# Add, layer normalization, one core: row statistics in two fixed sets of columns, one semaphore update for each four rows, one register value for all waits of a turn

## The chip, the cores and the metric

One core of a Trainium2 chip. The metric is the time of one execution on the device in microseconds (us). All runs told here were fast ones (granted clock 1.0). Before the change the median was 239.73 us of three runs (239.52 to 239.84).

## The reference

```python
# x, residual: float32 [16, 1024, 512]; gamma, beta: [512]; eps = 1e-5
z = x + residual
mean = np.mean(z, axis=-1, keepdims=True)
var = np.var(z, axis=-1, keepdims=True)
return gamma * (z - mean) / np.sqrt(var + eps) + beta
```

16,384 rows lie as 128 "rows" of 128 partitions, 512 values each; one such 128x512 row is 0.262 MB. All of `x` and `residual` is read once, all of the output written once: 100.67 MB.

## The kernel before

SP, POOL, ACT and DVE are engines of the core (SyncE, GpSimd, ScalarE and VectorE). SP issues every large transfer, on one queue. POOL adds `residual` to `x` in place, eight rows at a time. ACT takes the statistics of four rows (a "turn"): four Identity passes that sum into `nm` (minus the mean), four Square passes with that mean as bias that sum into `ssq`, one root. DVE takes two passes over each row, with a reciprocal between them. Each turn's statistics have columns of their own in `[P, total]` arrays, addressed by a register.

```python
Z_ROWS, R_ROWS, STORE_LAG, TURN = 64, 32, 40, 4
OUT_CHUNKS = [16] * 7 + [8, 4, 4]
...
    # SP: loads, and stores as rows are finished; a load into a used part of zbuf waits for its store
    for c, (lo, n) in enumerate(loads_x):
        ...
            wait_rows(s_out, "out", olo + on)
            move(dram(of, olo, on), part(zbuf, Z_ROWS, olo, on), so[oc])
    ...
    with act.Fori(0, turns) as t:
        zoff = act.snap((t * (TURN * D)) % (Z_ROWS * D))
        r0 = act.snap(t * TURN)
        act.wait_ge(s_add, r0 + TURN)
        for k in range(TURN):
            act.activation(out=junk_m[k][:, :], in_=zbuf[:, bass.ds(zoff + k * D, D)],
                           func=ACT.Identity, scale=-inv_d,
                           accum_out=nm[:, bass.ds(r0 + k, 1)]).then_inc(s_act, 1)
        act.wait_ge(s_act, r0 * 2 + TURN)
        for k in range(TURN):
            act.activation(out=junk_s[k][:, :], in_=zbuf[:, bass.ds(zoff + k * D, D)],
                           func=ACT.Square, bias=nm[:, bass.ds(r0 + k, 1)],
                           accum_out=ssq[:, bass.ds(r0 + k, 1)]).then_inc(s_act, 1)
        act.wait_ge(s_act, r0 * 2 + 2 * TURN)
        act.activation(out=std[:, bass.ds(r0, TURN)], in_=ssq[:, bass.ds(r0, TURN)],
                       func=ACT.Sqrt, bias=eps_t[:, 0:1], scale=inv_d).then_inc(s_std, TURN)
    ...
    with dve.Fori(0, turns) as t:
        ...
        dve.wait_ge(s_act, r0 * 2 + 2 * TURN)
        # four passes: row = (row + nm) * gamma
        dve.wait_ge(s_std, r0 + TURN)
        dve.reciprocal(out=rstd[...], in_=std[...]).then_inc(s_dve, TURN)
        dve.wait_ge(s_dve, r0 + TURN)
        # four passes: row = row * rstd + beta, each .then_inc(s_out, 1)
```

Of the kernel before, what the change touches and what calls it, by code (L numbers as in the profile page):

```python
# [8 lines left out]
FP32 = mybir.dt.float32  # L9
ACT = mybir.ActivationFunctionType  # L10
ALU = mybir.AluOpType
# [6 lines left out]
Z_ROWS = 64  # L18
# [5 lines left out]


TURN = 4


EARLY = 2
# [3 lines left out]
def kernel(  # L33
# [9 lines left out]
    nc = tc.nc  # L43
    P = nc.NUM_PARTITIONS
# [3 lines left out]
    N, D = xf.shape  # L48
    inv_d = 1.0 / float(D)
    total = N // P  # L50
    turns = total // TURN


    tc.close()
# [8 lines left out]
    def dram(t, lo, n):  # L63
# [5 lines left out]
    zbuf = nc.alloc_sbuf_tensor("zbuf", [P, Z_ROWS * D], FP32)  # L69
# [1 line left out]
    gb_row = nc.alloc_sbuf_tensor("gb_row", [1, 2 * D], FP32)  # L71
    ones = nc.alloc_sbuf_tensor("ones", [1, P], FP32)
    eps_t = nc.alloc_sbuf_tensor("eps_t", [P, 1], FP32)

    nm = nc.alloc_sbuf_tensor("nm", [P, total], FP32)
    ssq = nc.alloc_sbuf_tensor("ssq", [P, total], FP32)
    std = nc.alloc_sbuf_tensor("std", [P, total], FP32)
    rstd = nc.alloc_sbuf_tensor("rstd", [P, total], FP32)
    gamma_p = nc.alloc_psum_tensor("gamma_p", [P, D], FP32)
    beta_p = nc.alloc_psum_tensor("beta_p", [P, D], FP32)  # L80
    junk_m = [nc.alloc_psum_tensor(f"junk_m{i}", [P, D], FP32) for i in range(TURN)]
    junk_s = [nc.alloc_psum_tensor(f"junk_s{i}", [P, D], FP32) for i in range(6 - TURN)]
    junk_s += [
        nc.alloc_sbuf_tensor(f"junk_s{i}", [P, D], FP32) for i in range(6 - TURN, TURN)
    ]
# [3 lines left out]
    def sem(name):  # L89
        s = nc.alloc_semaphore(name)  # L90
        sems.append(s)
        return s
# [5 lines left out]
    s_const = sem("const")  # L98
    s_pe = sem("pe")
    s_add = sem("add")  # L100
    s_act = sem("act")
    s_std = sem("std")
    s_dve = sem("dve")
    s_out = sem("out")
    so = [sem(f"so{c}") for c in range(len(stores))]
# [3 lines left out]
    def part(buf, size, lo, n):  # L109
        assert lo % size + n <= size  # L110
        return buf[:, (lo % size) * D : (lo % size + n) * D]
# [60 lines left out]
    for c, (lo, n) in enumerate(loads_x):  # L172
        nc.gpsimd.wait_ge(sx[c], 16)
        for rc, (rlo, rn) in enumerate(loads_r):
            if lo <= rlo < lo + n:
                assert rlo + rn <= lo + n
                nc.gpsimd.wait_ge(sr[rc], 16)
                for a in range(rlo, rlo + rn, ADD):
# [3 lines left out]
                        out=z, in0=z, in1=part(rbuf, R_ROWS, a, an), op=ALU.add  # L182
                    ).then_inc(s_add, an)


    act = nc.scalar
    act.preload_act_table_set("sqrt_and_others")  # L187
    act.wait_ge(s_const, 2)
    with act.Fori(0, turns) as t:  # L189
        zoff = act.snap((t * (TURN * D)) % (Z_ROWS * D))  # L190
        r0 = act.snap(t * TURN)
        act.wait_ge(s_add, r0 + TURN)
        for k in range(TURN):
            act.activation(  # L194
                out=junk_m[k][:, :],
                in_=zbuf[:, bass.ds(zoff + k * D, D)],
                func=ACT.Identity,
                scale=-inv_d,
                accum_out=nm[:, bass.ds(r0 + k, 1)],
            ).then_inc(s_act, 1)  # L200
        act.wait_ge(s_act, r0 * 2 + TURN)  # L201
        for k in range(TURN):
            act.activation(  # L203
                out=junk_s[k][:, :],
                in_=zbuf[:, bass.ds(zoff + k * D, D)],
                func=ACT.Square,
                bias=nm[:, bass.ds(r0 + k, 1)],
                accum_out=ssq[:, bass.ds(r0 + k, 1)],
            ).then_inc(s_act, 1)
        act.wait_ge(s_act, r0 * 2 + 2 * TURN)  # L210
        act.activation(  # L211
            out=std[:, bass.ds(r0, TURN)],
            in_=ssq[:, bass.ds(r0, TURN)],
            func=ACT.Sqrt,
            bias=eps_t[:, 0:1],
            scale=inv_d,
        ).then_inc(s_std, TURN)


    dve = nc.vector  # L220
    dve.wait_ge(s_pe, 2)
    with dve.Fori(0, turns) as t:
        zoff = dve.snap((t * (TURN * D)) % (Z_ROWS * D))
        r0 = dve.snap(t * TURN)
        dve.wait_ge(s_act, r0 * 2 + 2 * TURN)
        for k in range(TURN):
            row = zbuf[:, bass.ds(zoff + k * D, D)]
            dve.scalar_tensor_tensor(  # L228
                out=row,
                in0=row,  # L230
                scalar=nm[:, bass.ds(r0 + k, 1)],
                in1=gamma_p[:, :],
                op0=ALU.add,
                op1=ALU.mult,
            )
        dve.wait_ge(s_std, r0 + TURN)
        dve.reciprocal(  # L237
            out=rstd[:, bass.ds(r0, TURN)], in_=std[:, bass.ds(r0, TURN)]
        ).then_inc(s_dve, TURN)
        dve.wait_ge(s_dve, r0 + TURN)  # L240
        for k in range(TURN):
            row = zbuf[:, bass.ds(zoff + k * D, D)]
            dve.scalar_tensor_tensor(  # L243
                out=row,
                in0=row,
                scalar=rstd[:, bass.ds(r0 + k, 1)],
                in1=beta_p[:, :],
                op0=ALU.mult,
                op1=ALU.add,
            ).then_inc(s_out, 1)  # L250


    blks = nc.main_func.blocks
# [43 lines left out]
```

## Time and profile before

| | before |
|---|---|
| time, median of 3 | 239.73 us |
| share of the span that the transfer queue fills | 99.1% of 16 engines |
| ACT busy; one ACT turn of four rows | 78%; 6.21 us |
| DVE busy | 74% |
| last store issued; span | 230.8; 238.4 us |

From the page of the kernel before: the span and instruction count, the load and store queue's share of the 16 transfer engines, the chain that ended last by engine, and three groups (busy us, mean ns of one, then idle us just before them and who ended it):

```profile
span 238.4 us, 1803 instructions
...
q1 hardware_dynamic: 6336, 100.67, 99.1%
...
ACT 38%; DMA 33%; issue 10%; POOL 7%; ACTq 5%; DVE 3%; SPq 1%; DVEq 0%; POOLq 0%
...
L194 ACT ACTIVATE junk_m<-zbuf 128x512 f32 x128 | 74.9, 585 | 28.5 <-POOL zbuf L181 23.3
L203 ACT ACTIVATE junk_s<-zbuf,nm 128x512 f32 x128 | 88.8, 694 | 3.9
L243 DVE SCALAR_TENSOR_TENSOR zbuf<-zbuf,rstd,beta_p 128x512 f32 x128 | 87.1, 744 | 1.1
...
```

The chain gives ACT 38%, more than any other, and ACT is busy 78%. The queue is at 99.1%. To see which binds, compare what a turn costs each: ACT's turn is read from its timeline (start, length, operation, idle before), from one root to the next:

```profile
...
123.18 0.19 ACT L194 ACTIVATION_READ_ACCUMULATOR junk_m<-zbuf  x1
123.49 0.69 ACT L203 ACTIVATE junk_s<-zbuf,nm 128x512 f32 x1
...
126.24 0.19 ACT L203 ACTIVATION_READ_ACCUMULATOR junk_s<-zbuf,nm  x1
126.54 0.30 ACT L211 ACTIVATE std<-ssq,eps_t  x1
127.02 0.60 ACT L194 ACTIVATE junk_m<-zbuf 128x512 f32 x1 [0.18 <-issue]
...
```

The next turn's first Identity starts at 127.02, this turn's started at 120.81: 6.21 us. The last accumulator read ends at 123.37 and the first Square starts at 123.49, a gap of 0.12; the root starts 0.11 after the squares' last read; 0.18 is idle at the loop's end. For the same four rows the transfers need 3 x 4 x 0.262 = 3.15 MB, 7.3 us at the 429 GB/s of the table below. ACT has time to spare, and the waits show it (us in total, times, longest; the longest wait for POOL, 17.5 us, is the one for the first sums of all, and 5.8 us lie after 110 us):

```profile
...
ACT junk_m L194 <- POOL zbuf L181: 23.3, 3, 17.5
...
ACT junk_m L194 <- issue: 5.2, 29, 0.2
...
```

The table by stretches (stretch, its length, then busy us and count of PE, PE loads, DVE, ACT and POOL, the clock, and the last two columns, DMA share and GB/s):

```profile
...
12.00:206.00 194.00, 0.00 (x0) 0.00 (x0) 154.93 (x252) 167.20 (x491) 135.03 (x16) 1.00 1.00 429
206.00:226.00 20.00, 0.00 (x0) 0.00 (x0) 17.38 (x29) 18.05 (x54) 6.97 (x2) 1.00 1.01 436
226.00:236.00 10.00, 0.00 (x0) 0.00 (x0) 4.75 (x8) 0.00 (x0) 0.00 (x0) 1.00 0.98 418
236.00:237.00 1.00, 0.00 (x0) 0.00 (x0) 0.00 (x0) 0.00 (x0) 0.00 (x0) 1.00 0.08 33
237.00:238.00 1.00, 0.00 (x0) 0.00 (x0) 0.00 (x0) 0.00 (x0) 0.00 (x0) 1.00 0.04 16
...
```

The issue of the last store, on SP's timeline:

```profile
...
230.81 0.33 SPq L138 DMA_DIRECT2D out_dram<-zbuf  x1
```

### The profile page before, as it was taken

The page shows a single profiled execution, that of the slowest core. Times are in us where ns is not written, and L with a number is a line of the kernel's source. Part 1 is how long each engine was busy: PE and PEld are TensorE (multiplying, and loading weights), DVE is VectorE, ACT ScalarE, POOL GpSimd, SP SyncE. Part 2 cuts the span into 40 slices and gives each one's busy share as a digit, 9 for nine tenths or more (in the row PEclk, how much of TensorE's full clock was granted, in tenths as well). Part 3 has the DMA queues.
Part 4 walks back from the last instruction along what each step waited for, and adds up shares of the span by engine and source line. Part 5 has one row for each costly group of instructions (what it writes and reads, how often), then busy time and mean ns, then how long its engine had stood idle before and what let it go on. Part 6 is the DMA issues. An engine that isn't in the chain of part 4 may idle for free.

```text
span 238.4 us, 1803 instructions
## 1 busy us (share of the span) xinstructions
PE 3.7 (2%) x4; PEld 1.2 (0%) x4; DVE 177.2 (74%) x290; ACT 186.5 (78%) x545; POOL 142.2 (60%) x21
## 2 busy tenths in 40 slices
PE   0600000000000000000000000000000000000000
PEld 0100000000000000000000000000000000000000
DVE  0000488888888889998888888887888648888870
ACT  2003999999999999999999999989997399999700
POOL 0098988989889407893088930889209892770000
DMA  8999999999999999999999999999999999999996
GB/s 308 438 429 415 437 437 429 426 423 437 429 429 418 440 434 426 459 434 396 429 429 429 434 429 429 426 470 434 390 434 418 434 440 408 472 434 434 390 425 257
DMA packets 6340, 100.67 MB, mean 422 GB/s; under 512 B 706, under 2 KB 706, under 8 KB 708
## 3 DMA queue, kind: packets, MB, share of 16 engines
q1 hardware_dynamic: 6336, 100.67, 99.1%
q10 hardware_dynamic: 4, 0.00, 0.0%
HBM read 67.11 MB, written 33.55 MB: 422 GB/s over the span
## 4 chain that ended last, share of the span: by engine, by line
ACT 38%; DMA 33%; issue 10%; POOL 7%; ACTq 5%; DVE 3%; SPq 1%; DVEq 0%; POOLq 0%
DMA rbuf<-in_residual_dram 21%; ACT junk_s L203 20%; ACT junk_m L194 18%; DMA out_dram<-zbuf 12%; POOL zbuf L181 7%; ACTq L194 2%; DVE zbuf L228 2%; DVE zbuf L243 1%; ACTq L203 1%; SPq L138 1%; ACTq L189 1%; ACT std L211 0%; ACTq L201 0%; ACTq L210 0%; DVEq L228 0%
## 5 line engine op out<-in xcount | busy, mean ns | idle before, releaser
L181 POOL TENSOR_TENSOR zbuf<-zbuf,rbuf 128x4096 f32<-128x4096 f32 (+1 forms) x17 | 142.0, 8353 | 70.9 <-DMA rbuf<-in_residual_dram 70.9
L228 DVE SCALAR_TENSOR_TENSOR zbuf<-zbuf,nm,gamma_p 128x512 f32 x128 | 87.1, 743 | 50.4 <-ACT junk_s L203 50.4
L194 ACT ACTIVATE junk_m<-zbuf 128x512 f32 x128 | 74.9, 585 | 28.5 <-POOL zbuf L181 23.3
L203 ACT ACTIVATE junk_s<-zbuf,nm 128x512 f32 x128 | 88.8, 694 | 3.9
L243 DVE SCALAR_TENSOR_TENSOR zbuf<-zbuf,rstd,beta_p 128x512 f32 x128 | 87.1, 744 | 1.1
L203 ACT ACTIVATION_READ_ACCUMULATOR junk_s<-zbuf,nm x128 | 23.9, 187 | 0.0
L194 ACT ACTIVATION_READ_ACCUMULATOR junk_m<-zbuf x128 | 23.9, 187 | 0.0
L211 ACT ACTIVATE std<-ssq,eps_t x32 | 9.5, 297 | 3.7
L237 DVE RECIPROCAL rstd<-std x32 | 5.4, 170 | 0.0
L187 ACT ACT_TABLE_LOAD x1 | 1.3, 1283 | 2.7 <-PEq L55 2.7
L123 PE MATMUL gamma_p<-gb_row,ones 1*128 1x512 f32 x2 | 2.0, 1122 | 7.3 <-DMA gb_row<-in_gamma_dram 7.3
L123 PE MATMUL beta_p<-gb_row,ones 1*128 1x512 f32 x2 | 1.9, 1056 | 0.0
L118 DVE MEMSET ones<- 1x128 f32 x1 | 0.2, 165 | 2.0 <-PEq L55 2.0
L123 PEld LDWEIGHTS beta_p<-gb_row,ones 1*128 1x128 f32 x2 | 0.7, 332 | 1.0 <-DMA gb_row<-in_beta_dram 0.5
L123 PEld LDWEIGHTS gamma_p<-gb_row,ones 1*128 1x128 f32 x2 | 0.5, 305 | 7.3 <-issue 7.3
L278 POOL MEMSET const-float32-0.0<- 128x1 f32 x1 | 0.1, 99 | 0.2 <-issue 0.2
L278 POOL MEMSET const-bfloat16-1.0<- 128x1 bf16 x1 | 0.1, 101 | 0.0
L278 POOL MEMSET const-uint8-127<- 128x1 uint8 x1 | 0.1, 101 | 0.0
L278 POOL MEMSET const-float32-1.0<- 128x1 f32 x1 | 0.1, 98 | 0.0
L119 DVE MEMSET eps_t<- 128x1 f32 x1 | 0.1, 59 | 0.0
## 6 DMA issues: line engine op xcount, KB each, us to landing
zbuf<-in_x_dram SPq DMA_DIRECT2D x15, 2048.0 KB, 32.8
rbuf<-in_residual_dram SPq DMA_DIRECT2D x15, 2048.0 KB, 30.1
out_dram<-zbuf SPq DMA_DIRECT2D x7, 4096.0 KB, 28.6
zbuf<-in_x_dram SPq DMA_DIRECT2D x2, 1024.0 KB, 32.6
rbuf<-in_residual_dram SPq DMA_DIRECT2D x2, 1024.0 KB, 34.6
out_dram<-zbuf SPq DMA_DIRECT2D x1, 2048.0 KB, 15.0
out_dram<-zbuf SPq DMA_DIRECT2D x2, 1024.0 KB, 9.4
gb_row<-in_gamma_dram ACTq DMA_DIRECT2D x1, 2.0 KB
```

What stands on the lines that cost most here:

```text
L123: nc.tensor.matmul(dest[:, :], ones[:, :], gb_row[:, k * D : (k + 1) * D], start=True, stop=True).then_inc(s_pe, 1)
L138: i = nc.sync.dma_start(out=out, in_=in_).then_inc(s, 16)
L181: nc.gpsimd.tensor_tensor(out=z, in0=z, in1=part(rbuf, R_ROWS, a, an), op=ALU.add).then_inc(s_add, an)
L187: act.preload_act_table_set("sqrt_and_others")
L189: with act.Fori(0, turns) as t:
L194: act.activation(out=junk_m[k][:, :], in_=zbuf[:, bass.ds(zoff + k * D, D)], func=ACT.Identity, scale=-inv_d, accum_out=nm[:, bass.ds(r0 + ...
L203: act.activation(out=junk_s[k][:, :], in_=zbuf[:, bass.ds(zoff + k * D, D)], func=ACT.Square, bias=nm[:, bass.ds(r0 + k, 1)], accum_out=ss ...
L211: act.activation(out=std[:, bass.ds(r0, TURN)], in_=ssq[:, bass.ds(r0, TURN)], func=ACT.Sqrt, bias=eps_t[:, 0:1], scale=inv_d,).then_inc(s ...
L228: dve.scalar_tensor_tensor(out=row, in0=row, scalar=nm[:, bass.ds(r0 + k, 1)], in1=gamma_p[:, :], op0=ALU.add, op1=ALU.mult,)
L237: dve.reciprocal(out=rstd[:, bass.ds(r0, TURN)], in_=std[:, bass.ds(r0, TURN)]).then_inc(s_dve, TURN)
L243: dve.scalar_tensor_tensor(out=row, in0=row, scalar=rstd[:, bass.ds(r0 + k, 1)], in1=beta_p[:, :], op0=ALU.mult, op1=ALU.add,).then_inc(s_ ...
L278: nc = _bacc.Bacc("TRN2", target_bir_lowering=False, num_devices=1)
```

## The change

Its intent: spare ACT and DVE the register work between their instructions. Statistics live in two sets of four columns at fixed addresses; the last row of four alone updates a semaphore; three separate semaphores count rows alike, so that one register value (`due`) serves every wait. As columns are reused, ACT must wait until DVE's reciprocal of two turns back is done. Two turns are written out in each pass of the loop.

```diff
+SETS = 2
+LAP = SETS * TURN
 ...
-    nm = nc.alloc_sbuf_tensor("nm", [P, total], FP32)      # and ssq, std, rstd
+    nm, ssq, std, rstd = (
+        [nc.alloc_sbuf_tensor(f"{name}{j}", [P, TURN], FP32) for j in range(SETS)]
+        for name in ("nm", "ssq", "std", "rstd")
+    )
 ...
-    with act.Fori(0, turns) as t:
-        zoff = act.snap((t * (TURN * D)) % (Z_ROWS * D))
-        r0 = act.snap(t * TURN)
-        act.wait_ge(s_add, r0 + TURN)
 ...
+    act.sem_inc(s_dve, LAP)
+    with act.Fori(0, total // LAP) as lap:
+        z0 = act.snap((lap * (LAP * D)) % (Z_ROWS * D))
+        r0 = act.snap(lap * LAP)
+        for j in range(SETS):
+            due = act.snap(r0 + (j + 1) * TURN)
+            act.wait_ge(s_dve, due)
+            act.wait_ge(s_add, due)
+            zk = [zbuf[:, bass.ds(z0 + (j * TURN + k) * D, D)] for k in range(TURN)]
+            for k in range(TURN):
+                i = act.activation(out=junk_m[k][:, :], in_=zk[k], func=ACT.Identity,
+                                   scale=-inv_d, accum_out=nm[j][:, k : k + 1])
+            i.then_inc(s_mean, TURN)
+            act.wait_ge(s_mean, due)
+            for k in range(TURN):
+                i = act.activation(out=junk_s[k][:, :], in_=zk[k], func=ACT.Square,
+                                   bias=nm[j][:, k : k + 1], accum_out=ssq[j][:, k : k + 1])
+            i.then_inc(s_ssq, TURN)
+            act.wait_ge(s_ssq, due)
+            # root of ssq[j] into std[j], .then_inc(s_std, TURN)
 ... DVE alike: waits s_ssq >= due, s_std >= due,
+            dve.reciprocal(out=rstd[j][:, :], in_=std[j][:, :]).then_inc(s_dve, TURN)
+            dve.wait_ge(s_dve, due + LAP)
 ... second pass over four rows, the last alone:
-            ).then_inc(s_out, 1)
+            i.then_inc(s_out, TURN)
```

More of the change, by code (lines that the diff above doesn't have):

```diff
@@ L50 @@
     total = N // P
-    turns = total // TURN
     tc.close()
@@ L73 @@
     eps_t = nc.alloc_sbuf_tensor("eps_t", [P, 1], FP32)
-    nm = nc.alloc_sbuf_tensor("nm", [P, total], FP32)
-    ssq = nc.alloc_sbuf_tensor("ssq", [P, total], FP32)
-    std = nc.alloc_sbuf_tensor("std", [P, total], FP32)
-    rstd = nc.alloc_sbuf_tensor("rstd", [P, total], FP32)
+    nm, ssq, std, rstd = (
+        [nc.alloc_sbuf_tensor(f"{name}{j}", [P, TURN], FP32) for j in range(SETS)]
+        for name in ("nm", "ssq", "std", "rstd")
+    )
     gamma_p = nc.alloc_psum_tensor("gamma_p", [P, D], FP32)
@@ L100 @@
     s_add = sem("add")
-    s_act = sem("act")
-    s_std = sem("std")
+    s_mean, s_ssq, s_std = sem("mean"), sem("ssq"), sem("std")
     s_dve = sem("dve")
@@ L188 @@
     act.wait_ge(s_const, 2)
-    with act.Fori(0, turns) as t:
-        zoff = act.snap((t * (TURN * D)) % (Z_ROWS * D))
-        r0 = act.snap(t * TURN)
-        act.wait_ge(s_add, r0 + TURN)
-        for k in range(TURN):
-            act.activation(
-                out=junk_m[k][:, :],
-                in_=zbuf[:, bass.ds(zoff + k * D, D)],
-                func=ACT.Identity,
-                scale=-inv_d,
-                accum_out=nm[:, bass.ds(r0 + k, 1)],
-            ).then_inc(s_act, 1)
-        act.wait_ge(s_act, r0 * 2 + TURN)
-        for k in range(TURN):
-            act.activation(
-                out=junk_s[k][:, :],
-                in_=zbuf[:, bass.ds(zoff + k * D, D)],
-                func=ACT.Square,
-                bias=nm[:, bass.ds(r0 + k, 1)],
-                accum_out=ssq[:, bass.ds(r0 + k, 1)],
-            ).then_inc(s_act, 1)
-        act.wait_ge(s_act, r0 * 2 + 2 * TURN)
-        act.activation(
-            out=std[:, bass.ds(r0, TURN)],
-            in_=ssq[:, bass.ds(r0, TURN)],
-            func=ACT.Sqrt,
-            bias=eps_t[:, 0:1],
-            scale=inv_d,
-        ).then_inc(s_std, TURN)
+    act.sem_inc(s_dve, LAP)
@@ new lines @@
+    with act.Fori(0, total // LAP) as lap:
[7 more added lines that the diff above has]
+            for k in range(TURN):
+                i = act.activation(
+                    out=junk_m[k][:, :],
+                    in_=zk[k],
+                    func=ACT.Identity,
+                    scale=-inv_d,
+                    accum_out=nm[j][:, k : k + 1],
+                )
+            i.then_inc(s_mean, TURN)
+            act.wait_ge(s_mean, due)
+            for k in range(TURN):
+                i = act.activation(
+                    out=junk_s[k][:, :],
+                    in_=zk[k],
+                    func=ACT.Square,
+                    bias=nm[j][:, k : k + 1],
+                    accum_out=ssq[j][:, k : k + 1],
+                )
+            i.then_inc(s_ssq, TURN)
+            act.wait_ge(s_ssq, due)
+            act.activation(
+                out=std[j][:, :],
+                in_=ssq[j][:, :],
+                func=ACT.Sqrt,
+                bias=eps_t[:, 0:1],
+                scale=inv_d,
+            ).then_inc(s_std, TURN)
@@ L220 @@
     dve = nc.vector
     dve.wait_ge(s_pe, 2)
-    with dve.Fori(0, turns) as t:
-        zoff = dve.snap((t * (TURN * D)) % (Z_ROWS * D))
-        r0 = dve.snap(t * TURN)
-        dve.wait_ge(s_act, r0 * 2 + 2 * TURN)
-        for k in range(TURN):
-            row = zbuf[:, bass.ds(zoff + k * D, D)]
-            dve.scalar_tensor_tensor(
-                out=row,
-                in0=row,
-                scalar=nm[:, bass.ds(r0 + k, 1)],
-                in1=gamma_p[:, :],
-                op0=ALU.add,
-                op1=ALU.mult,
-            )
-        dve.wait_ge(s_std, r0 + TURN)
-        dve.reciprocal(
-            out=rstd[:, bass.ds(r0, TURN)], in_=std[:, bass.ds(r0, TURN)]
-        ).then_inc(s_dve, TURN)
-        dve.wait_ge(s_dve, r0 + TURN)
-        for k in range(TURN):
-            row = zbuf[:, bass.ds(zoff + k * D, D)]
-            dve.scalar_tensor_tensor(
-                out=row,
-                in0=row,
-                scalar=rstd[:, bass.ds(r0 + k, 1)],
-                in1=beta_p[:, :],
-                op0=ALU.mult,
-                op1=ALU.add,
-            ).then_inc(s_out, 1)
+    with dve.Fori(0, total // LAP) as lap:
+        z0 = dve.snap((lap * (LAP * D)) % (Z_ROWS * D))
+        r0 = dve.snap(lap * LAP)
+        for j in range(SETS):
+            due = dve.snap(r0 + (j + 1) * TURN)
+            zk = [zbuf[:, bass.ds(z0 + (j * TURN + k) * D, D)] for k in range(TURN)]
+            dve.wait_ge(s_ssq, due)
+            for k in range(TURN):
+                dve.scalar_tensor_tensor(
+                    out=zk[k],
+                    in0=zk[k],
+                    scalar=nm[j][:, k : k + 1],
+                    in1=gamma_p[:, :],
+                    op0=ALU.add,
+                    op1=ALU.mult,
+                )
+            dve.wait_ge(s_std, due)
+            dve.reciprocal(out=rstd[j][:, :], in_=std[j][:, :]).then_inc(s_dve, TURN)
+            dve.wait_ge(s_dve, due + LAP)
+            for k in range(TURN):
+                i = dve.scalar_tensor_tensor(
+                    out=zk[k],
+                    in0=zk[k],
+                    scalar=rstd[j][:, k : k + 1],
+                    in1=beta_p[:, :],
+                    op0=ALU.mult,
+                    op1=ALU.add,
+                )
+            i.then_inc(s_out, TURN)
```

## The prediction

> **What bounds the kernel.** The transfers. The page gives the load/store queue 99.1% of the 16 DMA engines' span. In the table by stretches the DMA share is 1.00 at 429 GB/s from 12 to 206 us and 1.02 at 438 from 206 to 220. [...] 100.67 MB at 429 to 438 GB/s is 230 to 235 us (estimate); first bytes and the last store's completion (data stop at 236.1, end at 238.4) make up the rest. The chain of waits shows ACT at 38%, but ACT is second: a turn of four rows takes it 6.21 us (timeline, 120.81 to 127.02), while the transfers need 3 x 4 x 0.262 MB = 3.15 MB, 7.3 us at 429 GB/s.
>
> **What the change does.** The instruction order shows: on ACT the four row addresses per turn stay; four register operations at the squares, two ahead of the waits, one ahead of the root, and every second loop end go; waits for its own statistics now sit on the ACTIVATE itself. New: a wait for DVE's reciprocal two turns back. On DVE the reciprocal's address, three additions in the second pass and every second loop end go. No ACTIVATE, accumulator read or vector operation is added or removed.
> Costed from the timeline of one turn: of 6.21 us, 0.18 is idle at the loop end ("issue", 5.2 us over 29 turns in the waits); about 0.1 each is lost before squares and root, mostly the round trip of ACT's own results, which stays. [...] most of the 0.18 can go, with an overlap of 0.09 more. I expect a turn of 5.9 to 6.15 us (5.95), 2 to 10 us less ACT time in all. DVE (5.6 us busy per turn, 0.64 idle behind ACT) follows. The new wait costs nothing: that reciprocal ends about 3 us before it is asked for.
>
> **On the critical path.** Almost nothing. A faster ACT makes stores be asked for earlier, into a queue that is never dry: 4 MB stores take 28.6 us from issue to landing, against about 10 of transfer. The last store is issued at 230.8 and data move until 236.1: 5.3 us, of which its own 1.05 MB is 2.4. DMA share is 0.97 in 225 to 228 and 0.88 in 230 to 231: 0.2 to 0.3 us is all that an earlier last store can recover.
>
> **Prediction: 239.5 us, 80% range 238.8 to 240.1.** Faster by over 2%: 2%; within 2%: 97%; slower by over 2%: 1%.
>
> **Signs.** Right: queue share about 99%, 420 to 425 GB/s; ACT turn below 6.21, less "issue" idle before the mean ACTIVATE, more idle of ACT behind POOL; last store issued 0.5 to 2 us earlier, end moved under 0.5; busy time of ACT and DVE unchanged. Wrong: an ACT wait on DVE's reciprocal; an ACT turn over 6.5 us; a DMA share under 0.95 in any 10 us stretch.
>
> **What would make it wrong.** A longer ACT turn: the last store has about 1 us of slack (estimate), so even a few tenths more per turn would show in the tail. Or a transfer rate that depends on how loads and stores are mixed: an earlier store changes the mix, and the rate could move by a per cent.

What the transfers can do rests on the 429 to 438 GB/s of the trace. 6.21 us, less most of the 0.18 and the 0.09, came to a turn of 5.95 us. An overlap of 0.09 us as such is in the trace of the kernel before: an ACTIVATE starts at 121.44 while the accumulator read ahead of it ends at 121.53.

## More of the kernel before

Up to 236 us the transfers hardly pause. After that about one engine is left at work: 0.08 of sixteen engines is 1.3 engines, and 0.04 is 0.6.

## The result, and the profile after

The changed kernel takes 239.19 us (238.95 to 239.51, six runs); the kernel before, with three more runs of it, 239.62 us (239.48 to 239.84). The ratio is 0.9982, 95% interval 0.9969 to 0.9995: the same at 2%, a little faster at a finer look. (A ratio here is the mean time of one kernel's fast runs over that of the other's of the same rounds, so not quite the ratio of the medians quoted.)

The page of the changed kernel, the same lines:

```profile
span 237.9 us, 1484 instructions
...
q1 hardware_dynamic: 6336, 100.67, 99.3%
...
DMA 49%; ACT 24%; POOL 11%; DVE 5%; issue 4%; SPq 1%; ACTq 1%; DVEq 0%; POOLq 0%
...
L201 ACT ACTIVATE junk_m<-zbuf 128x512 f32 x128 | 74.8, 585 | 31.5 <-POOL zbuf L181 29.1
L211 ACT ACTIVATE junk_s<-zbuf,nm 128x512 f32 x128 | 88.9, 695 | 1.0
L251 DVE SCALAR_TENSOR_TENSOR zbuf<-zbuf,rstd,beta_p 128x512 f32 x128 | 87.1, 743 | 1.1
...
```

Busy times per operation are as before to a nanosecond or two. The count of instructions falls from 1803 to 1484. The chain now names DMA first, 49% to ACT's 24%, although the bound has not changed: a chain jumps through whichever wait came last, and a small shift of ACT turned many of those waits.

ACT's timeline, over one turn that begins behind a loop end (117.14) and ends without one (122.99):

```profile
...
116.64 0.30 ACT L220 ACTIVATE std<-ssq,eps_t 128x4 f32<-128x4 f32 x1
117.14 0.60 ACT L201 ACTIVATE junk_m<-zbuf 128x512 f32 x1 [0.20 <-issue]
...
119.51 0.19 ACT L201 ACTIVATION_READ_ACCUMULATOR junk_m<-zbuf 128x1 f32 x1
119.73 0.69 ACT L211 ACTIVATE junk_s<-zbuf,nm 128x512 f32 x1
...
122.47 0.19 ACT L211 ACTIVATION_READ_ACCUMULATOR junk_s<-zbuf,nm 128x1 f32 x1
122.75 0.30 ACT L220 ACTIVATE std<-ssq,eps_t 128x4 f32<-128x4 f32 x1
122.99 0.60 ACT L201 ACTIVATE junk_m<-zbuf 128x512 f32 x1
```

The gap before the first Square is 0.03 (119.70 to 119.73), was 0.12; that before the root is 0.09, was 0.11. The turn that follows inside the loop starts at 122.99 with no idle, even 0.06 before the root has ended, while the loop end (117.14) keeps 0.20 us. Two turns take 11.97 us (turns start at 63.16 and, four later, at 87.10), 12.42 before (59.98 and 84.81). The waits of ACT:

```profile
...
ACT junk_m L201 <- POOL zbuf L181: 29.1, 4, 17.4
...
ACT junk_m L201 <- issue: 2.4, 12, 0.2
...
```

Of what ACT saved, 5.8 us came back as more waiting for POOL's sums, which wait for loads. And the transfers:

```profile
...
12.00:206.00 194.00, 0.00 (x0) 0.00 (x0) 155.15 (x253) 167.07 (x494) 135.39 (x16) 1.00 1.01 429
206.00:226.00 20.00, 0.00 (x0) 0.00 (x0) 18.85 (x31) 17.19 (x51) 6.62 (x2) 1.00 1.02 437
226.00:236.00 10.00, 0.00 (x0) 0.00 (x0) 3.04 (x6) 0.00 (x0) 0.00 (x0) 1.00 0.97 414
236.00:237.00 1.00, 0.00 (x0) 0.00 (x0) 0.00 (x0) 0.00 (x0) 0.00 (x0) 1.00 0.10 41
237.00:238.00 1.00, 0.00 (x0) 0.00 (x0) 0.00 (x0) 0.00 (x0) 0.00 (x0) 1.00 0.02 8
...
```

The rates in the first three stretches are those of before within 1% (429, 437 and 414 GB/s for 429, 436 and 418), so the prediction's other worry, a rate that moves with the mix of loads and stores, did not show. The last store was asked for 1.7 us earlier:

```profile
...
229.10 0.33 SPq L138 DMA_DIRECT2D out_dram<-zbuf  x1
```

The end of the span came 0.5 us earlier, and in this trace the difference lies where the sixteen engines finish. In the traces of both kernels each of the 44 large transfers has sixteen landings (a landing is an update of the transfer's semaphore that the trace lists with it), spread over 0.35 to 2.18 us. As the page counts sixteen engines, and the last two microseconds show the work of about one (0.08 and 0.04 of sixteen above), I take each landing for the end of one engine's share; that is a reading. Of the last store, in us from the start of the span, first, median, last but one and last landing (taken from the kept traces; no view of the profile lists them):

```
                   first   median   15th    16th
before             236.15  236.42  236.81  238.33
changed            236.08  236.54  237.15  237.86
```

Fifteen engines end no sooner with the change. One engine lags, and it lags less: behind the median landing by 1.91 us before and by 1.32 with the change (there the fifteenth is late too). The traces give the landings without the number of the engine, so that it is one and the same engine all along is not shown. The lag builds up during the run: before the change the sixteenth landing came 0.07 us after the fifteenth for the first load, 0.58 for a store that landed at 169 us, 1.52 for the last store. It grows in steps, and before the change each step lies across a store: behind the median landing it is about 0.2 us over the first fourteen loads, 0.36, 0.63, 0.87, 1.12 and 1.33 us for the loads that follow each of the first five stores, and it stands still over the loads in between.

### The profile page after: what moved, and what is told of

Same layout as the page of the kernel before. It is cut to its first block, busy times and chain, and to the rows that moved or that the text cites. A ratio compares the mean times of both kernels' runs of the same rounds, so it can differ in the third digit from the quotient of the medians.

```text
span 237.9 us, 1484 instructions
## 1 busy us (share of the span) xinstructions
PE 3.7 (2%) x4; PEld 1.2 (0%) x4; DVE 177.2 (74%) x290; ACT 185.5 (78%) x545; POOL 142.2 (60%) x21
## 4 chain that ended last, share of the span: by engine, by line
DMA 49%; ACT 24%; POOL 11%; DVE 5%; issue 4%; SPq 1%; ACTq 1%; DVEq 0%; POOLq 0%
DMA rbuf<-in_residual_dram 36%; ACT junk_s L211 14%; DMA out_dram<-zbuf 13%; POOL zbuf L181 11%; ACT junk_m L201 10%; DVE zbuf L239 3%; DVE zbuf L251 3%; SPq L138 1%; ACTq L201 1%; DVEq L239 0%; ACT std L220 0%; DVE rstd L248 0%; ACTq L192 0%; ACTq L198 0%; DVEq L231 0%
## 5 line engine op out<-in xcount | busy, mean ns | idle before, releaser
L211 ACT ACTIVATION_READ_ACCUMULATOR junk_s<-zbuf,nm 128x1 f32 x128 | 23.9, 187 | 0.0
L201 ACT ACTIVATION_READ_ACCUMULATOR junk_m<-zbuf 128x1 f32 x128 | 23.9, 186 | 0.0
L220 ACT ACTIVATE std<-ssq,eps_t 128x4 f32<-128x4 f32 x32 | 9.5, 297 | 3.0
L248 DVE RECIPROCAL rstd<-std 128x4 f32<-128x4 f32 x32 | 5.4, 170 | 0.0
```

Source lines behind the costliest of these rows:

```text
L201: i = act.activation(out=junk_m[k][:, :], in_=zk[k], func=ACT.Identity, scale=-inv_d, accum_out=nm[j][:, k : k + 1],)
L211: i = act.activation(out=junk_s[k][:, :], in_=zk[k], func=ACT.Square, bias=nm[j][:, k : k + 1], accum_out=ssq[j][:, k : k + 1],)
L220: act.activation(out=std[j][:, :], in_=ssq[j][:, :], func=ACT.Sqrt, bias=eps_t[:, 0:1], scale=inv_d,).then_inc(s_std, TURN)
L248: dve.reciprocal(out=rstd[j][:, :], in_=std[j][:, :]).then_inc(s_dve, TURN)
```

## The experiments

Theory 1: the transfers bind; ACT's time has nowhere to show. Theory 2: ACT's chain binds, as the chain of waits before the change suggested, and the gain was small because ACT gained little. Each run below is against runs of the kernel before on the same chip, five rounds. Three chips were used, on which the kernel before takes 239.7, 239.81 and 240.07 us.

### narrow: ACT's passes cut to a quarter

```diff
-                    out=junk_m[k][:, :], in_=zk[k],        # Identity; the Square alike
-                    scale=-inv_d,
+                    out=junk_m[k][:, 0:128], in_=zk[k][:, 0:128],
+                    scale=-inv_d * 4.0,
```

> The changed kernel with both statistics taken over the first 128 of the 512 columns, scales adapted (on purpose a wrong result); loads, stores, adds and DVE as in the changed kernel. An ACT turn should fall from about 5.98 to 3.4 us (eight passes shorter by about 0.32 us each). Theory 1 (the transfers bound the kernel; a faster ACT only fills the few tenths of idle transfer time at the end): time 238.6 to 239.4, thus within 0.5 us of the changed kernel. Theory 2 (ACT's chain bounds it, as the chain of waits suggests): the 82 us of ACT time saved would show, the time falls by 5 us or more. If theory 1 holds and the time is still some tenths below the changed kernel, the end had more to give than the change took.

Measured: 239.33 us, ratio 0.9988 (0.9975 to 1.0001). Wrong result on purpose. ACT's busy time between 12 and 206 us fell from 167 to 96 us, and all of it became waiting (one Identity follows another after 0.29 us, 129.23 to 129.52, where the changed kernel has 0.61, 117.77 to 118.38):

```profile
...
ACT junk_m L201 <- POOL zbuf L181: 94.7, 15, 17.4
...
ACT junk_m L201 <- DVE rstd L248: 11.1, 6, 2.2
...
```

(Where nothing else holds ACT up, the new wait for DVE's reciprocal shows too, 11.1 us of it.) The long stretch of the table, and the issue of the last store:

```profile
...
12.00:206.00 194.00, 0.00 (x0) 0.00 (x0) 156.77 (x259) 96.37 (x510) 135.11 (x16) 1.00 1.01 429
...
224.01 0.33 SPq L138 DMA_DIRECT2D out_dram<-zbuf  x1
```

The transfers run at the same 429 GB/s. The last store was issued at 224.0 us, 5.1 earlier than in the changed kernel, and the time is no lower. Theory 2 falls. So does the prediction's small term: there was nothing at the end for an earlier last store to recover.

### fewer_loads: two of seventeen residual loads left out

```diff
+SKIP = (6, 10)
+            if rc in SKIP:
+                continue
             wait_rows(s_add, "add", rlo + rn - R_ROWS)
             move(part(rbuf, R_ROWS, rlo, rn), dram(rf, rlo, rn), sr[rc])
 ... and POOL doesn't wait for those two
```

> The changed kernel without two of the seventeen loads of the residual (the two chunks' sums then use old rows, on purpose a wrong result); all else the same. 4.19 MB less at 429 GB/s is 9.8 us. Theory 1: the time falls by 8.5 to 10 us, to 229 to 231 (ACT alone would allow 22 + 32 x 5.98 and some 12 for the last rows, about 226). Theory 2: it stays within 2 us of 239.2.

Measured: 229.53 us, ratio 0.9583, 10.2 us less than the kernel before and 9.7 less than the changed one; 4.19 MB at 429 GB/s is 9.8. Theory 1 holds in size as well. (Wrong result on purpose.)

### slow1: one more ACT pass per turn

```diff
+            i = act.activation(out=junk_x[:, :], in_=zk[0], func=ACT.Identity)
             i.then_inc(s_mean, TURN)
```

> The changed kernel with one more pass (Identity, 128x512, no sum) per turn on ACT, into a buffer of its own; right result. An ACT turn becomes about 6.5 us, 32 x 0.52 = 16.6 us more in all. Theory 1: ACT had slack of 5.6 us of idle in the middle, about 1 us of slack at the last store, and so it only just becomes the limit: 22 + 32 x 6.5 + 5.6 for DVE's last turn + 6 for the last store is 241.5 of span, time 241 to 244. Theory 2: the time grows by all 16.6, to 255 to 256.

Measured: 240.16 us (240.11 to 240.21), ratio 1.0020 (1.0007 to 1.0033). Neither figure: far below theory 2's 255, and below the 241 to 244 that I worked out for theory 1. The ACT turn from 119.00 to 125.64 takes 6.64 us, 0.53 more than the 6.11 of such a turn in the changed kernel. SP issued the last store at 234.93:

```profile
...
234.93 0.33 SPq L139 DMA_DIRECT2D out_dram<-zbuf  x1
```

and the transfers around it:

```profile
...
233.00:234.00 1.00, 0.00 (x0) 0.00 (x0) 1.00 (x2) 0.00 (x0) 0.00 (x0) 1.00 0.46 188
234.00:235.00 1.00, 0.00 (x0) 0.00 (x0) 0.91 (x2) 0.00 (x0) 0.00 (x0) 1.00 0.06 25
235.00:235.75 0.75, 0.00 (x0) 0.00 (x0) 0.00 (x0) 0.00 (x0) 0.00 (x0) 1.00 0.03 11
235.75:236.00 0.25, 0.00 (x0) 0.00 (x0) 0.00 (x0) 0.00 (x0) 0.00 (x0) 1.00 1.26 524
236.00:237.00 1.00, 0.00 (x0) 0.00 (x0) 0.00 (x0) 0.00 (x0) 0.00 (x0) 1.00 0.93 393
...
```

Here the queue does run dry, from before 234 to 235.75: this is what ACT on the critical path looks like. Data of the last store begin 0.8 us after its issue (234.93 to about 235.75), and all sixteen landings fall within 0.2 us (238.61 to 238.82), 3.9 us after the issue. I had put 6 us. Two things follow. First, the slack in the kernel before: the last store was issued at 230.81, its data could begin at 231.6; the stores ahead of it kept the engines until about 236.1 - 2.4 = 233.7 (estimate; 2.4 is its own 1.05 MB at 429 GB/s). So it had about 2.1 us of slack, not the 1 us of the prediction, and the changed kernel about 3.8. Second, the pause lets the lagging engine catch up (the sixteenth landing comes 0.01 us after the fifteenth, here and at the end of tight_wait): the median landing is 2.3 us later than before the change (238.72 for 236.42), the sixteenth only 0.5 (238.82 for 238.33), and the sixteenth is what ends the run.

### unroll: two turns per loop pass, nothing else

```diff
-    with act.Fori(0, turns) as t:                # DVE alike
+    with act.Fori(0, turns // 2) as lap:
+        z0 = act.snap((lap * (2 * TURN * D)) % (Z_ROWS * D))
+        q0 = act.snap(lap * (2 * TURN))
+        for j in range(2):                       # body as before, zoff = z0 + j * TURN * D, r0 = q0 + j * TURN
```

> The kernel before with nothing but two turns written out in each pass of the ACT and DVE loops; columns still addressed, one semaphore update per row, a wait value for each wait. If the loop end is what the change saved on ACT, every second idle of 0.18 us goes (and its overlap of 0.07), so two turns take 12.15 to 12.2 us against 12.42 before and 11.96 after; the gaps of 0.12 before the squares and 0.11 before the root stay. If the addressed columns and wait values were the saving, two turns stay at 12.4. Time under theory 1: 239.2 to 239.7 either way.

Measured: 239.62 us, ratio 1.0001 (0.9986 to 1.0016). Two turns on ACT take 12.23 us (59.91 to 84.37 is two pairs). So the loop end is worth 0.19 of the 0.45 us that the change saves per two turns.

### addressed: the changed kernel with addressed columns

```diff
-                    accum_out=nm[j][:, k : k + 1],
+                    accum_out=nm[:, bass.ds(r0 + j * TURN + k, 1)],     # ssq, std, rstd alike, [P, total]
-            act.wait_ge(s_dve, due)
```

> The changed kernel (two turns per loop pass, one update for each four rows, one register value for all waits) but with the statistics again in addressed columns, one for each row of the input; the wait for DVE's reciprocal is not needed and goes. Measured so far per two turns on ACT: 12.42 us before, 12.23 with the loops alone written out, 11.97 changed. Reading A (the 0.26 us between the last two come from addressing columns: a register operation carries the wait ahead of squares and root): the gaps before the squares and the root stay near 0.12 and 0.11, two turns take 12.2. Reading B (they come from the wait values): the gaps fall to 0.03 and 0.09, two turns take 12.0. Time under theory 1 (transfers bound it): 239.0 to 239.7 either way.

Measured: 239.43 us, ratio 0.9977 (0.9964 to 0.9989); the kernel before ran at 240.07 on this chip. Two turns take 12.30 us. ACT's timeline:

```profile
...
110.29 0.19 ACT L198 ACTIVATION_READ_ACCUMULATOR junk_m<-zbuf  x1
110.60 0.69 ACT L208 ACTIVATE junk_s<-zbuf,nm 128x512 f32 x1
...
113.34 0.19 ACT L208 ACTIVATION_READ_ACCUMULATOR junk_s<-zbuf,nm  x1
113.65 0.30 ACT L217 ACTIVATE std<-ssq,eps_t  x1
113.85 0.60 ACT L198 ACTIVATE junk_m<-zbuf 128x512 f32 x1
...
```

110.48 to 110.60 and 113.53 to 113.65: both gaps are 0.12 again. Reading A is right: the addressed column makes the wait sit on a register operation ahead of the ACTIVATE (in the trace of the kernel before, one for the squares' wait stands at 123.40, ahead of the Square at 123.49), and that costs 0.09 us per batch of squares (the gap is 0.03 in the changed kernel, whose trace has the wait on the Square itself). The 12.30 is more than the 12.2 expected: in the other turn of each pass the gap before the root is 0.20, and the idle at the loop end is 0.24 for 0.20. Sharing one wait value saved nothing that the turn shows.

### tight_wait: the new wait one turn tighter

```diff
-    act.sem_inc(s_dve, LAP)
+    act.sem_inc(s_dve, TURN)
-            dve.wait_ge(s_dve, due + LAP)
+            dve.wait_ge(s_dve, due + TURN)
```

> The changed kernel with the new wait one turn tighter, as a single set of columns would need it: ACT starts a turn only when DVE's reciprocal of the turn just before it is done. Right result. Reading A (the new wait is real, and two sets are what makes it free): from the end of ACT's squares 0.2 + 2.64 + 0.17 us of DVE and about 0.15 to get going lie between, so a turn takes about 5.52 + 3.15 = 8.65 us, more than the 7.3 us that the transfers need for four rows, and ACT becomes the bound: 22 + 32 x 8.65 + about 6 for the last rows + 1.3 outside the span, 302 to 311 us. Reading B (the wait overlaps even so): under 245 us.

Measured: 305.98 us, ratio 1.2743. ACT turns take 8.65 us (64.57, 73.21, 81.86, ...), to the hundredth as expected, and the wait shows by name:

```profile
...
ACT junk_m L201 <- DVE rstd L248: 84.8, 31, 2.7
...
ACT junk_m L201 <- POOL zbuf L181: 17.3, 1, 17.3
...
```

The changed kernel's list of waits has no such line. A wait as tight as one set of columns needs makes ACT the bound; the second set is what makes reuse free. A single set itself was not run: to be free of races it would need one more wait, for `rstd`, so this stands in for it.

### four_sets

Only `SETS = 4`.

> The changed kernel with four sets of columns: four turns written out per loop pass, the wait four turns back. Three of four loop ends without the 0.2 us idle: four turns on ACT about 23.7 us against 23.94. Theory 1: no gain, 238.9 to 239.5. A rival that credits the changed kernel's 0.4 us to its shorter ACT turn (0.45 us per two turns) expects another 0.2 us less, 239.0 or below.

Measured: 239.88 us median (239.11 to 240.22, six runs), ratio 0.9984 (0.9968 to 1.0000), on the chip where the kernel before is at 240.07. Four turns take 23.76 us (23.94 with two sets). The median lies above both expectations, which were made from times on another chip; the ratio is that of the changed kernel. No further gain from ACT shows.

### after_again: the changed kernel once more

> The changed kernel itself once more, to see how much of its 0.43 us against the kernel before comes again. If the gain is a property of the change: ratio 0.997 to 0.9995 again. If it is spread between runs (one transfer engine of sixteen lags by 0.7 to 1.5 us behind the last but one at the end, differently in each trace): ratio 0.9995 to 1.001.

Measured: 239.25 us, ratio 0.9970 (0.9956 to 0.9983). The small gain comes again (that it is larger here is not shown, as the two intervals overlap). So it wanted a cause, and neither ACT's turn (unroll, four_sets) nor the issue of the last store (narrow) was it.

### last_on_15: the last store in two parts

```diff
+                move(d[0:120, :], z[0:120, :], so[oc])
+                move(d[120:P, :], z[120:P, :], so[oc])
-    nc.sync.wait_ge(so[-1], 16)
+    nc.sync.wait_ge(so[-1], 32)
```

> The changed kernel with its last store in two parts, 120 partitions (a multiple of 15) and 8. In all traces so far one of the sixteen landings of the last store comes 0.7 to 1.5 us after the one before it, so one transfer engine sets the end. If a part of 120 partitions uses fifteen of the engines and the lagging one is the one left out, it has 2.4 us less to do, the others up to 0.3 us more, and the time falls by 0.5 to 1.0 us, to 238.2 to 238.7. If the lagging engine is another one, the time stays at 239.2 to 239.6.

Measured: 240.00 us, ratio 1.0017 (0.9999 to 1.0036). A miss. ("In all traces so far" was too wide: slow1 and tight_wait have 0.01 us there.) The trace has 23 landings of data on that semaphore, as fifteen engines for one part and eight for the other would give. Two of them came late, at 238.20 and 238.51, the one before them at 237.49. Two late landings, one for each part, fit a lagging engine that served both parts and was not the one spared. No version better than the changed kernel came of it.

### row_updates: an update per row again

```diff
-                )
-            i.then_inc(s_mean, TURN)      # s_ssq and s_out alike
+                ).then_inc(s_mean, 1)
```

> The changed kernel with a semaphore update for each row again (mean, squares and finished rows), all else as changed. If updates cost ACT time, two turns take more than the 11.97 us of the changed kernel, up to 0.03 per update, 12.2; if they are free, 11.97 within 0.02. Time under theory 1: 239.0 to 239.6 either way.

Measured: 239.50 us, ratio 0.9993 (0.9980 to 1.0006). Two turns take 11.97 us (63.32 to 87.25 is two pairs): updates cost ACT nothing. The time lies nearer to the kernel before than to the changed one, but its interval holds both.

### thin_before and more_updates

By now the kernels with many semaphore updates seemed the slower ones, whatever ACT did. Two runs ask that. thin_before is the kernel before with

```diff
-            ).then_inc(s_act, 1)          # s_out alike
+            )
+            if k == TURN - 1:
+                i.then_inc(s_act, TURN)
```

> The kernel before with one semaphore update for each four rows (mean, squares, finished rows) and nothing else: columns stay addressed, one turn per loop pass. So far the kernels with an update per row stand at ratios 1.0001 and 0.9993 to the kernel before, those with an update for each four rows at 0.9970 to 0.9988, whatever their ACT turn (11.97 with one update per row gives 0.9993, 12.30 with one for four rows gives 0.9977). Reading S (the updates themselves, 465 before and 177 after, slow the transfers' lagging engine a little): ratio 0.9970 to 0.9988. Reading N (that sorting is chance within the spread of runs): 0.9993 to 1.0010. The ACT turn should stay at 6.21 us.

and more_updates is the changed kernel with

```diff
+    s_spare = sem("spare")
+    with pe.Fori(0, 16) as g:
+        pe.wait_ge(s_add, pe.snap(g * 8 + 8))
+        for _ in range(60):
+            pe.sem_inc(s_spare, 1)
 ...
+    nc.sync.wait_ge(s_spare, 960)
```

> The changed kernel with 960 more semaphore updates, in 16 bursts of 60 by the otherwise idle PE sequencer, spread over the run, on a semaphore that nothing but the end waits for. Reading S: 288 updates fewer went with 0.4 to 0.8 us, so 960 more cost 1.4 to 2.7 us: 240.6 to 242. Reading N: no change from the changed kernel, 239.0 to 239.6 (0.3 us more where this chip's kernel before is slower too).

Measured: thin_before 239.53 us, ratio 0.9993 (0.9979 to 1.0006), which by itself fits either reading; its ACT turn stayed at 6.21. more_updates 240.84 us, ratio 1.0047 (1.0033 to 1.0060), within what reading S expected. The transfers' last stretch:

```profile
...
236.00:237.00 1.00, 0.00 (x0) 0.00 (x0) 0.00 (x0) 0.00 (x0) 0.00 (x0) 1.00 0.13 49
237.00:238.00 1.00, 0.00 (x0) 0.00 (x0) 0.00 (x0) 0.00 (x0) 0.00 (x0) 1.00 0.06 25
...
```

One engine is at work longer than before or after. Its landings say it plainly: first 236.11, median 236.40, fifteenth 236.78, sixteenth 239.13. Fifteen engines end when they always do; one is 2.35 us late. Updates and instructions that touch no data made one transfer engine lag by more (2.73 us behind the median landing, 1.32 in the changed kernel).

Put beside all kernels whose bytes and bound are alike. "Events" are the instructions that the page counts and the semaphore updates in the same trace, added:

| kernel | instructions + updates = events | ratio to before |
|---|---|---|
| more_updates | 2494 + 2200 = 4694 | 1.0047 |
| before | 1803 + 1527 = 3330 | 1 |
| unroll | 1739 + 1530 = 3269 | 1.0001 |
| thin_before | 1803 + 1239 = 3042 | 0.9993 |
| row_updates | 1484 + 1531 = 3015 | 0.9993 |
| addressed | 1643 + 1239 = 2882 | 0.9977 |
| narrow | 1484 + 1242 = 2726 | 0.9988 |
| changed, twice | 1484 + 1240 = 2724 | 0.9982, 0.9970 |
| four_sets | 1452 + 1241 = 2693 | 0.9984 |

A straight line through these ten has a slope of 3.4 millionths per event (correlation 0.96), about 0.8 ns; without more_updates the slope is the same (3.5, correlation 0.82). The change takes away 606 events, which the line makes 0.2%, 0.5 us: what was measured, 0.18% and 0.30%. ACT's turn does not give this order (narrow has the shortest).

Three cautions. Each ratio has an interval of about 0.0013 to either side, so only more_updates stands clear of its neighbours. The ratios come from different chips; on the one chip of unroll, thin_before, narrow and more_updates the order is the same to 0.0001. And last_on_15 is left out because its last store is another one; with its 2731 events and 1.0017 it would lie far above the line, and the correlation without more_updates would be 0.39.

The kept traces say more than these ratios. The lag of the last landing behind the median one, one trace each, is 2.73 us with 2494 instructions (more_updates), 1.91 and 1.84 with 1803 (before and thin_before, 1527 and 1239 updates), 1.48 with 1739 (unroll), 1.43 with 1643 (addressed) and 1.16 to 1.36 with 1484 (changed twice, narrow and row_updates, 1240 to 1531 updates). So in these traces the lag goes with the instructions; 290 updates more or less move it by 0.04 to 0.20 us. Only four_sets does not fit: 2.13 us with 1452. A rival is that the fetching of instructions takes the time. The traces list these packets: none after the first transfer in the kernel before, and one each in the changed kernel (0.01 MB on its page) and in more_updates, so they can't explain the order of these three. They seem to cost something: in unroll the lag grew by 0.35 us where a single one, of 8 KB and 0.33 us, ran at 34 us, and two in four_sets go with 0.59 of its lag. Another 0.62 of it came near 130 us, with no such packet and no store, and has no known cause.

## Why the prediction was right

The time fell inside the range (239.19 for 239.5, 238.8 to 240.1), and its main steps held.

- "The transfers" bind: shown. Cutting ACT's work to a fraction left the time (narrow), taking away 4.19 MB took 9.7 to 10.2 us (fewer_loads).
- An ACT turn of 5.95 us: measured 5.98 as the mean of eight turns, 5.85 and 6.11 alternating. The sum had one wrong term, though: "mostly the round trip of ACT's own results, which stays". The gap before the squares went from 0.12 to 0.03; it was a register operation carrying the wait (addressed), and ACT's own result comes back within 0.03. (Before the root, 0.09 of 0.11 did stay.) The loop end gave less than hoped, since every second one stays at 0.20.
- "The new wait costs nothing": shown from both sides, by its absence after the change and by 84.8 us of it in tight_wait.
- "Almost nothing" on the critical path: right. But the term "0.2 to 0.3 us is all that an earlier last store can recover" named the wrong place. The last store already had about 2.1 us of slack, and asking for it 5.1 us earlier still (narrow) gave nothing. The small gain that was measured, 0.43 us, lies in one lagging transfer engine (sixteenth landing at 237.86 for 238.33, the median no earlier), and goes, as far as the table and the traces show, with the number of instructions and updates that the program executes. That the gain of 0.2 to 0.3 us in the prediction came near it is luck: it was to come from a different place.

What stays open: why. No run shows in what way instructions and updates would hold up one transfer engine. A steady charge for each of them would make the lag grow over the loads as well, where it stands still in the kernel before (0.63 us behind the median for each of the four loads that landed from 115 to 130 us); each step there lies across a store, but whether it takes a store to bring one, no run asked. And no run here was made without the profiler, so it is not shown that an unprofiled execution has the lag or the gain at all. Which of instructions and updates counts for more, the times do not say; the traces point to the instructions.

## What to carry to other kernels

When one resource is full at every moment, judge other engines by what they need per unit of work (ACT 6.2 us, transfers 7.3 us for four rows) and not by their share of the chain of waits, and look for their slack at the last transfer. Fixed addresses and a wait that sits on the compute instruction itself shortened ACT's turn here (0.26 of 12.42 us, and two turns per loop pass another 0.19), and two sets of columns made reuse free where the wait that one set needs cost 66 us. It should pay where that engine is the bound, which no run here shows. At differences of a few tenths of a per cent, read the end of the last transfer engine by engine before crediting a gain to the part that was changed.
